# Layer 0's attention on one Trainium2 core, its five instruction queues ordered by a table instead of by a scheduler

## The chip, the cores and the metric

One core of one Trainium2 chip runs the kernel. The core has five engines that work side by side, each through its own queue of instructions and in the order of that queue: TensorE (PE in the profile; its weight loads are PEld), VectorE (DVE), ScalarE (ACT), GpSimd (POOL) and SyncE (SP), which issues the DMA transfers. The metric is the device time of one execution in microseconds (us).

## The reference

Two blocks stand one behind the other, for 1024 tokens of width 1024. The first has two layers (differential attention, then MLA); the second has three mixers and a feed-forward part. The change touches layer 0, which cut to its core is this:

```
h = rmsnorm(x, g) * (1 + scale) + shift          # shift, scale, gate: silu(c) @ ada_w + ada_b
q, k, v, z = split(h @ w_in)                     # w_in 1024 x 4096; 8 heads of 128
q, k = rope(q), rope(k)                          # 2 maps of 64 in each head
sc = einsum('bqhcd,bkhcd->bhcqk', q, k) * scale
p = softmax(sc);  p = p[:, :, 0] - lam * p[:, :, 1]
o = einsum('bhqk,bkhd->bqhd', p, v)
o = rmsnorm(o, subln_g) * (1 - lambda_init) * silu(z)
x = x + gate * (o @ w_out)
```

Layer 1 then starts with its own rmsnorm, shift and scale, and a product with its w_in.

## The kernel before, in words

Products of fp32 numbers are made of three products of a high and a low part each (`mm3`, line 198: hi x hi, hi x lo, lo x hi), so a product of 1024 rows of weights with 512 tokens is 24 matmuls of 512 columns. `wload` (line 185) loads a weight block into a tile wr, casts its high part on ACT (wh, L195) and subtracts the low part on POOL (wl, L181). The activations h are kept as such pairs, in two halves of 512 tokens.

Layer 0's attention goes through 8 heads of 8 tiles (128 queries each), 64 steps (`da_attention`, line 895). A step makes the scores of a tile for both maps (`da_softmax`, line 869: 8 matmuls into two tiles s, a maximum on DVE L760, an exponential on ACT L764, a reciprocal on DVE L879, a scaling on POOL L881, the combination of the two maps on DVE L882). LAG = 2 steps later the tile is transposed on PE (`pt_fill`, L174: 8 transposes, then casts on ACT L783 and subtractions on DVE L181), and after four tiles they are multiplied with v (24 matmuls, `da_stat`), normed (a sum by two matmuls, L410, L411, L920), gated with silu(z) and stored to od by a DMA (L822). Beside that run the products of v and z of the head and of q and k of the next (`qk_rope`, line 637). Its rope is four DVE operations and a POOL addition (L627 to L631); the split pair ab is spread to kk and qq by 32 small DMAs per head (L693). A modulation row of layer 0 and three of layer 1 are summed up in chunks of a loaded weight tile on DVE (L335).

What sets the order: the program hands over its instructions with priorities, and a scheduler puts them on the queues. Only PE's matmuls and transposes are kept in program order there (`self.pin`, `pinned`, line 167); the attention is written ahead by `HP_A` priorities, and generators mix the rest between its steps:

```
fill = alternate(chain(v(h, b2), qk(h + 1, heads[h + 1][0]), z(h, b2)), some(late, 5 if h else 8))
merge(some(att, 8), fill, 0 if h else LEAD0)
```

Behind the last head come the output projection (`out_proj`, line 794; its inputs are the heads loaded back from od by `load_o`, L816 splits them), for half 0 and then half 1, the sum of squares over the result (`stat_sum`, L400), and layer 1's h (`make_h`). There layer 1 starts with two z blocks. PSUM has 8 banks here: two tiles s of two banks, and four tiles m of one bank for all else.

## Time and profile before

| | |
|---|---|
| runs of the kernel before, us | 2951.8 (median of 3; 2949.33 to 2963.5) |
| the profiled execution, us | 2957.26 |
| its span, us (first to last instruction) | 2955.4 |
| mean granted clock of TensorE | 0.949 |
| busy of the span: PE / PEld | 89% / 73% |
| DVE / ACT / POOL | 72% / 48% / 44% |
| mean DMA rate | 115 GB/s |

Times are in us from the start of the span. Layer 0's first scores start at 103, the last head's at 690; its output projection runs from about 776 to 888, layer 1 follows. The granted clock is a share of full speed. A row of a timeline gives start, duration, engine, line, operation, output<-input and count; in brackets stands the idle time of the engine just before, and who ended it.

### The profile page before, as it was taken

How to read it: one execution, taken by the hardware profiler on the slowest of the kernel's cores; microseconds unless marked ns; L12 is line 12 of the kernel's file. 1: busy time of each engine (PE TensorE's matmuls, PEld its weight loads, DVE VectorE, ACT ScalarE, POOL GpSimd, SP SyncE). 2: the span in 40 equal slices, each digit the busy share in tenths (PEclk: the TensorE clock that was granted, in tenths of full speed). 3: DMA queues.
4: the chain of work that ended last, by engine and by line, in shares of the span. 5: the costliest groups of instructions: out<-in, count | busy, mean ns of one | idle time of the engine just before them, and what ended most of it. 6: DMA issues, size and time to landing. Idle time of an engine off the chain costs nothing. (4 is left out here: it accounts for less than half of the span.)

```text
span 2955.4 us, 34418 instructions
## 1 busy us (share of the span) xinstructions
PE 2643.0 (89%) x12023; PEld 2143.1 (73%) x12023; DVE 2117.6 (72%) x2696; ACT 1429.1 (48%) x2609; POOL 1302.3 (44%) x779
## 2 busy tenths in 40 slices
PE   7789999998889989999997798887887999998897
PEld 4667777786768767787775577776775777776775
DVE  7678878776552477676767555568868888889865
ACT  5355545555534544554554344467544444443432
POOL 3333333234244342222233332244537887778761
PEclk8999999999999989999998899999999999998998
DMA  7533433323351264233432336424441222234564
GB/s 269 146 101 83 125 86 85 88 68 111 96 169 58 73 230 137 90 111 94 142 111 69 101 80 91 101 73 117 135 147 50 79 79 75 85 107 154 192 233 145
DMA packets 316849, 338.90 MB, mean 115 GB/s; under 512 B 37684, under 2 KB 240516, under 8 KB 316676
## 3 DMA queue, kind: packets, MB, share of 16 engines
q1 hardware_dynamic: 316676, 336.70, 38.7%
q8 instruction: 96, 1.57, 0.2%
q14 instruction: 77, 0.63, 0.1%
HBM read 231.17 MB, written 60.89 MB: 99 GB/s over the span
## 5 line engine op out<-in xcount | busy, mean ns | idle before, releaser
L171 PE MATMUL m<-h,wh 128*128 128x512 f32 x4744 | 1398.1, 405 | 78.4 <-ACT wh L195 15.8
L171 PEld LDWEIGHTS m<-h,wh 128*128 128x128 f32 x4744 | 915.8, 195 | 288.2 <-ACT wh L195 16.7
L171 PE MATMUL m<-h,wl 128*128 128x512 f32 x1472 | 590.7, 403 | 9.7 <-POOL wl L181 9.7
L181 POOL TENSOR_TENSOR wl<-wr,wh 128x1024 fp32r<-128x1024 f32 (+1 forms) x146 | 328.9, 2259 | 475.6 <-ACT wh L195 144.5
L171 PEld LDWEIGHTS m<-h,wl 128*128 128x128 f32 x1472 | 287.8, 196 | 74.9 <-POOL wl L181 12.1
L783 ACT CAST pt<-m 128x256 fp32r<-128x256 f32 (+1 forms) x632 | 218.6, 373 | 237.9 <-PE m L174 134.7
L764 ACT ACTIVATE e<-s,cf 128x1024 f32<-128x1024 f32 x192 | 215.2, 1122 | 190.8 <-DVE cf L760 87.7
L181 DVE TENSOR_TENSOR pt<-m,pt 128x256 fp32r<-128x256 f32 (+2 forms) x652 | 254.0, 415 | 65.2 <-ACT pt L783 53.5
L760 DVE TENSOR_REDUCE cf<-s 128x1 f32<-128x1024 f32 x192 | 229.6, 1215 | 53.0 <-PE s L171 53.0
L171 PE MATMUL m<-pt,v 128*128 128x512 f32 (+3 forms) x1052 | 240.4, 376 | 15.3 <-ACT pt L1493 9.9
L881 POOL TENSOR_SCALAR e<-e,cf 128x1024 f32<-128x1024 f32 x64 | 84.0, 1313 | 344.9 <-DVE cf L879 291.6
L171 PEld LDWEIGHTS m<-pt,v 128*128 128x128 f32 x1052 | 189.2, 192 | 55.5 <-ACT pt L1493 11.3
L171 PE MATMUL s<-kk,qq 128*128 128x512 f32 (+3 forms) x752 | 191.1, 391 | 41.0 <-DVE e L1417 17.5
L171 PE MATMUL s<-h,wh 128*128 128x512 f32 x720 | 183.7, 401 | 34.3 <-DVE h L181 16.8
L174 PE MATMUL m<-cr,e 128*128 128x128 f32 x1314 | 193.0, 279 | 17.8 <-DVE pt L181 11.6
L1607 DVE SCALAR_TENSOR_TENSOR e<-z,cf,e 128x1023 f32<-128x1023 f32 (+1 forms) x88 | 175.8, 2009 | 24.8 <-ACT e L1605 24.6
L171 PEld LDWEIGHTS s<-kk,qq 128*128 128x128 f32 x752 | 136.8, 198 | 73.5 <-DVE e L1417 20.4
L174 PEld LDWEIGHTS m<-cr,e 128*128 128x128 f32 x1314 | 157.7, 143 | 43.3 <-issue 14.9
L171 PEld LDWEIGHTS s<-h,wh 128*128 128x128 f32 x720 | 137.1, 192 | 70.4 <-DVE h L181 18.5
L171 PE MATMUL s<-h,h 128*128 128x512 f32 x640 | 167.3, 408 | 18.8 <-DVE h L181 11.4
L195 ACT CAST wh<-wr 128x1024 fp32r<-128x1024 f32 (+2 forms) x134 | 122.0, 914 | 112.2 <-PE m L171 48.8
L171 PEld LDWEIGHTS s<-h,h 128*128 128x128 f32 x640 | 121.1, 194 | 49.4 <-DVE h L181 13.3
(343 smaller groups left out, 4087.9 us busy)
## 6 DMA issues: line engine op xcount, KB each, us to landing
wr<-in_w_out_dram SPq DMA_DIRECT2D x48, 512.0 KB
tb<-in_w_ada_dram SPq DMA_DIRECT2D x48, 512.0 KB
wr<-in_w_up_dram SPq DMA_DIRECT2D x47, 512.0 KB
wr<-in_w_in_dram SPq DMA_DIRECT2D x45, 512.0 KB
qq<-ab SPq DMA_DIRECT2D x144, 128.0 KB
wr<-in_ada_w_dram SPq DMA_DIRECT2D x32, 512.0 KB
tf<-act SPq DMA_DIRECT2D x30, 512.0 KB
wr<-in_w_down_dram SPq DMA_DIRECT2D x30, 512.0 KB
```

Of the source, the lines that this page charges most:

```text
L171: return self.pinned(self.nc.tensor.matmul(*args, **kw))
L174: return self.pinned(self.nc.tensor.transpose(*args))
L181: (eng or self.nc.vector).tensor_sub(lo, src, hi.bitcast(F32))
L195: nc.scalar.copy(hi, raw)
L760: nc.vector.reduce_max(nm, ps, axis=AX, negate=True)
L764: nc.scalar.activation(e, ps, AF.Exp, bias=nm, scale=scale, accum_out=sm)
L783: nc.scalar.copy(hi, ps[:, i:i + m])
L881: nc.gpsimd.tensor_scalar(e1, e1, sm[:, 1:2], self.neglam, ALU.mult, ALU.mult)
L1607: nc.vector.scalar_tensor_tensor(t[:, sh:], u[:, 0:S - sh], col(i), t[:, sh:], ALU.mult, ALU.add)
```

## The change

All five engines are wrapped (`Engine`), so that every instruction issued while `self.pin` is set keeps its program order on its queue. `at(g, place, fn)` enters a piece of work in a table under a step g and a place in the step; `run_table` emits the table in the order of steps and places, from step -4 to 82. A product becomes a `unit`: 12 matmuls at place 60, 12 at place 80 of its step, its result read in the next step; the four transposes of each half tile stand at places 50 and 70. v stands in a head's steps 0 and 1, q and k of the next head in steps 2 to 5, z of the next head in steps 6 and 7 (the last head's own v and z in 56 to 59; z of head 0 in steps -2 and -1), and the products with v in step 6 and step 2 of the next head. The output projection takes steps 64 to 79, three z blocks of layer 1 (half 0) steps 80 to 82. Transposes and sums go to two PSUM tiles t, products to two tiles u, in this stretch in place of the four m. wr has 5 buffers where it had 2 (phase 0), wl of phase 1 has 3 where it had 2. The q and k columns of w_in0 are laid out anew by the host, so that one DMA loads q and k of 512 rows in rows of 1 KB, where there were two with 512 bytes, and the cast reads straight. Two small loads of column vectors move to steps 9 and 17. The diff, cut to its core:

```diff
-LEAD0 = 2
...
-    dict(h4=20, kk=5, qq=5, ab=2, pt=12, e=6, v=3, z=3, wr=2, wh=3, wl=3, tb=3, t2=4, tf=3),
-    dict(h4=18, kk=4, qq=6, ab=3, pt=12, e=6, v=3, z=3, wr=4, wh=3, wl=2, tb=3, t2=2, tf=4),
+    dict(h4=20, kk=5, qq=5, ab=2, pt=12, e=6, v=3, z=3, wr=5, wh=3, wl=3, tb=3, t2=4, tf=3),
+    dict(h4=18, kk=4, qq=6, ab=3, pt=12, e=6, v=3, z=3, wr=4, wh=3, wl=3, tb=3, t2=2, tf=4),
...
+    def __getattr__(self, name):
+        f = getattr(self.engine, name)
+
+        def call(*args, **kw):
+            ins = f(*args, **kw)
+            return self.net.tc.keep_in_program_order(ins) if self.net.pin else ins
+
+        return call
...
+    def pt(self, shape=(128, 512)):
+        self.n += 1
+        return self.ps_t.tile(list(shape), F32, tag="t", name=f"t_{self.n}")
+
+    def pu(self, shape=(128, 512)):
+        self.n += 1
+        return self.ps_u.tile(list(shape), F32, tag="u", name=f"u_{self.n}")
...
-            for i, c0 in enumerate((qcol, kcol)):
-                nc.sync.dma_start(
-                    raw[:, :, i], w[g * 512:g * 512 + 512, c0:c0 + 128].rearrange("(k p) m -> p k m", p=128))
-            src = raw.rearrange("p k q (s i f) -> p i (k q s) f", s=2, i=2)
-            h, l = (x.rearrange("p i k (s f) -> p i (k s) f", f=32) for x in (hi, lo))
+            rows = lambda c0, n: w[g * 512:g * 512 + 512, c0:c0 + n].rearrange("(k p) m -> p k m", p=128)
+            if kcol is None:
+                nc.sync.dma_start(raw.rearrange("p k q m -> p k (q m)"), rows(qcol, 256))
+                src = raw.rearrange("p k i m -> p i k m")
+                h, l = hi, lo
+            else:
+                for i, c0 in enumerate((qcol, kcol)):
+                    nc.sync.dma_start(raw[:, :, i], rows(c0, 128))
+                src = raw.rearrange("p k q (s i f) -> p i (k q s) f", s=2, i=2)
+                h, l = (x.rearrange("p i k (s f) -> p i (k s) f", f=32) for x in (hi, lo))
...
+    def at(self, g, place, fn, *args, phase=0):
+        self.table.setdefault(g, []).append((place, len(self.table.get(g, ())), fn, args, phase))
+
+    def run_table(self):
+        self.pin = True
+        for g in range(min(self.table), max(self.table) + 1):
+            for _, _, fn, args, self.phase in sorted(self.table.get(g, ()), key=lambda e: e[:2]):
+                fn(*args)
+        self.pin = False
+        self.phase = 0
...
+    def weight_block(self, g, srcs, chunks, phase=0, late=0):
+
+
+        nc = self.nc
+        ws, box = [], []
+
+        def load():
+            raw = self.load("wr", [128, 1024])
+            for dst, src in srcs(raw):
+                nc.sync.dma_start(dst, src)
+            box.append(raw)
+
+        def first():
+            hi = self.t("wh", [128, 1024], F32R)
+            nc.scalar.copy(hi, box[0])
+            box.append(hi)
+
+        def rest():
+            raw, hi = box
+            lo = self.t("wl", [128, 1024], F32R)
+            self.lo(lo, raw, hi, nc.gpsimd)
+            ws.extend(zip(chunks(hi), chunks(lo)))
+
+        self.at(g - (3 if late < 0 else 2), 11, load, phase=phase)
+        self.at(*((g, 9) if late > 0 else (g - 1 + late, 57)), first, phase=phase)
+        self.at(*((g, 35) if late > 0 else (g - 1 + late, 67)), rest, phase=phase)
+        return ws
...
+    def unit(self, g, ws, rs, read, phase=0, place=10):
+
+        box = []
+
+        def part(i):
+            if i == 0:
+                box.append(self.pu())
+            sl = slice(4 * i, 4 * i + 4)
+            self.mm3(box[0], ws()[sl], rs()[sl], start=i == 0, stop=i == 1)
+
+        self.at(g, 60, part, 0, phase=phase)
+        self.at(g, 80, part, 1, phase=phase)
+        self.at(g + 1, place, lambda: read(box[0]), phase=phase)
...
+            self.unit(g + half, lambda: ws, lambda half=half: hts[half], lambda ps, half=half: read(half, ps))
+            self.at(g + 2, (58, 90)[half], turns, half)
...
+        self.at(g + 2, 90, abs_exp)
+        self.at(g + 3, 58, ln)
+        self.at(g + 3, 91, both)
+        self.at(g + 4, 11, exp)
+        self.at(g + 4, 37, mul)
...
+            for qk in (1, 0):
+                for s in range(2):
+                    for d in range(2):
+                        for i in range(2):
+                            r = slice(64 * d + 32 * i, 64 * d + 32 * i + 32)
+                            x = slice(64 * qk + 32 * s, 64 * qk + 32 * s + 32)
+                            if qk:
+                                self.move(kk[s][r, half * 512:half * 512 + 512], ab[i][x, d])
+                            else:
+                                self.move(q[s][r], ab[i][x])
+
+        for half in range(2):
+            for i in range(2):
+                self.unit(g + 2 * half + i, lambda i=i: [(h[:, i], l[:, i]) for y in ws for h, l in y],
+                          lambda half=half: hts[half], lambda ps, half=half, i=i: read(half, i, ps), place=34)
+            self.at(*((g + 4, 90) if half else (g + 3, 56)), parts, half)
+            self.at(g + 4 + half, 12, moves, half)
...
+        self.at(n, 30, scores)
+        self.at(n, 32, exp, 0)
+        self.at(n, 52, exp, 1)
+        self.at(n, 65, sums)
+        self.at(n + 1, 33, combine)
+        self.at(n + LAG, 50, turns, 0)
+        self.at(n + LAG, 70, turns, 1)
...
+        self.at(g, 55, product)
+        self.at(g + 1, 10, read)
+        if h == 7:
+            self.at(g + 1, 85, sums)
+            self.at(g + 2, 11, ln)
+            self.at(g + 2, 11, exp)
+            self.at(g + 2, 34, scale)
+            self.at(g + 2, 36, gated)
+        else:
+            self.at(g + 2, 45, sums)
+            self.at(g + 2, 51, ln)
+            self.at(g + 2, 59, exp)
+            self.at(g + 2 + 2 * half, 92, scale)
+            self.at(g + 5 - half, 93 + half, gated)
+            self.at(g + 6 - half, 12, put)
...
+        self.at(g, 12, load)
+        self.at(g + 1, 90, keep)
...
+                self.at(g - 1, 96, load, w, grp, k, n)
+                self.at(g, 93, chunk, k, n, name)
+                n += 1
+            self.at(g + 1, 91, end, name, b, grp)
...
+        self.at(g - 2, 12, load)
+        for n in range(8):
+            ws = self.plain_block(g + n, w[:, n * 128:(n + 1) * 128], 0, -1)
+            self.unit(g + n, lambda ws=ws: ws, lambda: ots[half], lambda ps, n=n: read(n, ps))
+            if n % 2:
+                self.at(g + n + 2, 12, store, n)
...
+        self.at(g, 20, parts)
+        self.at(g, 72, sums)
+        for c in range(8):
+            self.at(g + c // per, 90 if per < 8 else 94, chunk, c)
...
+        for h in range(8):
+            g = 8 * h
+            block = lambda i: w[:, i * 1024 + h * 128:i * 1024 + h * 128 + 128]
+            self.da_z(g - 2 if h == 0 else g + 6 if h < 7 else g + 2, block(3), hts, zs[h])
+            self.da_v(g, block(2), hts, vs[h])
+            if h < 7:
+                self.da_qk(g + 2, w, h + 1, hts, kks[h + 1], qts[h + 1])
+            for half in range(2):
+                pts = []
+                for j in range(4):
+                    self.da_tile(g + 4 * half + j, kks[h], lambda h=h, half=half: qts[h][half], pts)
+                self.da_output(h, half, vs[h], pts, zs[h], od, ots)
...
+        steps = [g for g in range(66) if g % 8 in (0, 2, 6, 7)]
+        self.da_mods(steps, cs, [(a["ada_w0"], self.col["ada_b0"], 2, "gate0")] + [
+            (a["ada_w1"], self.col["ada_b1"], i, nme) for i, nme in ((1, "scale1"), (0, "shift1"), (2, "gate1"))])
+        for i, c in enumerate(((0, 1), (2, 3), (4, 5), (6,))):
+            self.da_chunks(56 + i if i < 3 else 62, od, 0, c, ots)
+            self.da_chunks(64 + i, od, 1, c, ots)
...
+        for half, tags in enumerate((("kk", "kk", "ab", "ab"), ("pt",) * 4)):
+            g = 64 + 8 * half
+            self.da_project(g, a["w_out0"], ots, lambda: self.mod["gate0"], xs0, self.xs1, half, tags, acc, xbox[half])
+            self.da_next(g + 8, (3, 8)[half], half, acc, xbox[half], lambda: (cols["a"], self.mod["shift1"]), h1[half])
+        wss, z1 = [], []
+        for i in range(3):
+            g = 80 + i
+            c = 704 + i * 128
+            ws = self.plain_block(g, a["w_in1"][:, c:c + 128], 1, -1)
...
+            self.unit(g, lambda ws=ws: ws, lambda: h1[0], read, 1)
+        self.run_table()
+        return h1, (wss, z1)
...
+    w = given["w_in0"]
+    qk = w[:, :2048].reshape(D, 2, 8, 2, 2, 32).transpose(0, 2, 4, 1, 3, 5).reshape(D, 2048)
+    given["w_in0"] = np.concatenate([qk, w[:, 2048:]], axis=1)
```

Three places, as the queues stand before and now. First PE in step 9 and its like (s scores, cr<-e transposes, h with wh, wl a product). Before:

```order
L171 MATMUL m_1564<-h_84_585,wh_1555 128x512 x2
L171 MATMUL m_1564<-h_84_585,wl_1556 128x512
L171 MATMUL s_1594<-kk_963,qq_1050 128x512 x4
L171 MATMUL s_1602<-kk_964,qq_1059 128x512 x4
L174 MATMUL m_1613<-cr,e_1478 128x128 x4
L174 MATMUL m_1622<-cr,e_1478 128x128 x4
L171 MATMUL m_1631<-h_86_591,wh_1555 128x512 x2
```

With the change:

```order
L111 MATMUL s_1564<-kk_1314,qq_1316 128x512 x4
L111 MATMUL t_1573<-cr,e_1451 128x128 x4
L111 MATMUL u_1586<-h_86_597,wh_1465 128x512 x2
L111 MATMUL u_1586<-h_86_597,wl_1469 128x512
L111 MATMUL u_1586<-h_87_601,wh_1465 128x512 x2
L111 MATMUL u_1586<-h_87_601,wl_1469 128x512
L111 MATMUL u_1586<-h_89_607,wh_1465 128x512 x2
L111 MATMUL u_1586<-h_89_607,wl_1469 128x512
L111 MATMUL u_1586<-h_90_611,wh_1465 128x512 x2
L111 MATMUL u_1586<-h_90_611,wl_1469 128x512
L111 MATMUL t_1603<-cr,e_1451 128x128 x4
L111 MATMUL u_1586<-h_92_617,wh_1465 128x512 x2
```

The two groups of four transposes stood together; now half a product stands between them, and the second half behind them.

Second SP where the second half of the next head's k and q is spread (kk, qq from ab), at the end of a head. Before:

```order
L693 DMA kk_964<-ab_1206 32x512
L693 DMA kk_964<-ab_1207 32x512
L693 DMA qq_1219<-ab_1206 32x1024 x2
L693 DMA qq_1219<-ab_1207 32x1024 x2
L693 DMA qq_1228<-ab_1206 32x1024
L645 DMA wr_1749<-in_w_in_dram 128x4x128 x2
L693 DMA qq_1228<-ab_1206 32x1024
L693 DMA qq_1228<-ab_1207 32x1024
L645 DMA wr_1756<-in_w_in_dram 128x4x128 x2
L693 DMA qq_1228<-ab_1207 32x1024
L325 DMA wr_1788<-in_ada_w_dram 128x1024
L822 DMA od_638<-t_226_1443 128x512
```

With the change (step 7 of head 1):

```order
L111 DMA qq_1978<-ab_1926 32x1024
L111 DMA wr_2102<-in_ada_w_dram 128x1024
L111 DMA od_644<-t_282_1746 128x512
L111 DMA kk_1975<-ab_2093 32x512
L111 DMA kk_1975<-ab_2094 32x512
L111 DMA kk_1975<-ab_2093 32x512
L111 DMA kk_1975<-ab_2094 32x512
L111 DMA kk_1976<-ab_2093 32x512
L111 DMA kk_1976<-ab_2094 32x512
L111 DMA kk_1976<-ab_2093 32x512
L111 DMA kk_1976<-ab_2094 32x512
L111 DMA qq_2113<-ab_2093 32x1024
```

Weight loads stood among the last moves; now a modulation load and the store of a head's output (od) stand ahead of all 16, the 8 of k go first, and nothing stands among them.

Third PE where the sum of squares of layer 0's half 0 is taken (tf,cr), in the output projection. Before:

```order
L171 MATMUL m_6797<-h_1022_6251,wh_6791 128x512 x2
L171 MATMUL m_6797<-h_1022_6251,wl_6792 128x512
L171 MATMUL m_6797<-h_1032_6326,wh_6791 128x512 x2
L171 MATMUL m_6797<-h_1032_6326,wl_6792 128x512
L171 MATMUL m_6797<-h_1055_6431,wh_6791 128x512 x2
L171 MATMUL m_6797<-h_1055_6431,wl_6792 128x512
L171 MATMUL m_6852<-tf_6849,cr 128x512
L171 MATMUL m_6911<-h_1106_6785,wh_6905 128x512 x2
L171 MATMUL m_6911<-h_1106_6785,wl_6906 128x512
L171 MATMUL m_6911<-h_1107_6788,wh_6905 128x512 x2
```

With the change (step 72):

```order
L111 MATMUL u_6867<-h_1084_6571,wl_6806 128x512
L111 MATMUL u_6867<-h_1092_6636,wh_6791 128x512 x2
L111 MATMUL u_6867<-h_1092_6636,wl_6806 128x512
L111 MATMUL u_6867<-h_1093_6639,wh_6791 128x512 x2
L111 MATMUL u_6867<-h_1093_6639,wl_6806 128x512
L111 MATMUL t_6882<-tf_6862,cr 128x512 x2
L111 MATMUL u_6867<-h_1103_6689,wh_6791 128x512 x2
L111 MATMUL u_6867<-h_1103_6689,wl_6806 128x512
L111 MATMUL u_6867<-h_1104_6692,wh_6791 128x512 x2
L111 MATMUL u_6867<-h_1104_6692,wl_6806 128x512
L111 MATMUL u_6867<-h_1111_6737,wh_6791 128x512 x2
L111 MATMUL u_6867<-h_1111_6737,wl_6806 128x512
```

The sum stood ahead of the product of half 1 (its second matmul further down, in that product); both its matmuls now stand in the middle of the product.

## Rows read from the trace of the kernel before

**Rows 1.** Windows: busy (count) of PE, PEld, DVE, ACT, POOL; granted clock; DMA share, GB/s.

```profile
117.00:671.00 554.00, 522.01 (x2476) 429.38 (x2475) 438.50 (x597) 301.21 (x593) 183.58 (x99) 0.98 0.34 92
671.00:776.00 105.00, 88.58 (x400) 71.29 (x399) 74.56 (x103) 64.15 (x125) 35.85 (x20) 0.93 0.35 106
776.00:836.00 60.00, 48.19 (x211) 39.15 (x210) 20.71 (x34) 22.24 (x37) 18.63 (x8) 0.92 0.43 127
836.00:888.00 52.00, 46.74 (x195) 37.52 (x195) 31.86 (x30) 21.97 (x32) 29.50 (x18) 0.96 0.54 162
1060.00:1110.00 50.00, 36.49 (x144) 28.56 (x142) 40.73 (x46) 17.15 (x32) 13.88 (x9) 0.80 0.76 247
```

**Rows 2.** Timeline of PE, 199 to 223 us.

```profile
199.82 1.03 PE L174 MATMUL m<-cr,e 128*128 128x128 f32 x8
200.61 0.72 PE L171 MATMUL m<-h,wh 128*128 128x512 f32 x2
...
208.48 5.61 PE L171 MATMUL m<-pt,v 128*128 128x512 f32 x24
213.93 1.04 PE L174 MATMUL m<-cr,e 128*128 128x128 f32 x8
...
216.60 0.73 PE L171 MATMUL m<-h,wh 128*128 128x512 f32 x2 [0.59 <-DVE v L181]
...
222.18 1.98 PE L171 MATMUL s<-kk,qq 128*128 128x512 f32 x8
```

**Rows 3.** Windows of PE's instructions of line L171 alone (512-column matmuls).

```profile
117.00:671.00 554.00, 477.63 (x1980) 0.98 0.34 92
671.00:776.00 105.00, 79.95 (x310) 0.93 0.35 106
776.00:836.00 60.00, 46.95 (x195) 0.92 0.43 127
```

**Rows 4.** Timeline of PE, 181 to 194 us.

```profile
181.30 3.71 PE L171 MATMUL s<-kk,qq 128*128 128x512 f32 x8
...
190.87 0.99 PE L171 MATMUL m<-h,wh 128*128 128x512 f32 x2 [4.54 <-DVE pt L181]
...
192.09 1.05 PE L171 MATMUL m<-h,wh 128*128 128x512 f32 x2
...
193.37 1.05 PE L171 MATMUL m<-h,wh 128*128 128x512 f32 x2
```

**Rows 5.** Timelines of ACT and of PE at the sum of half 0.

```profile
832.50 1.14 ACT L816 CAST h<-tf 128x512 fp32r<-128x512 f32 x2 [4.82 <-DMA tf<-od]
...
835.58 0.80 PE L171 MATMUL m<-tf,cr 128*128 128x512 f32 x1 [9.42 <-ACT tf L400]
```

**Rows 6.** Timelines of SP (DMA issues), DVE and PE before head 7's first scores.

```profile
677.39 4.99 SPq L693 DMA_DIRECT2D kk<-ab  x8
682.48 4.99 SPq L693 DMA_DIRECT2D qq<-ab  x8
...
684.38 1.28 DVE L882 SCALAR_TENSOR_TENSOR e<-e,cf,e 128x1024 f32<-128x1024 f32 x1
...
690.51 1.98 PE L171 MATMUL s<-kk,qq 128*128 128x512 f32 x8
```

**Rows 7.** Groups by line and shape, 100 to 760 us: busy, mean ns | idle before, releasers.

```profile
L760 DVE TENSOR_REDUCE cf<-s 128x1 f32<-128x1024 f32 x126 | 149.3, 1212 | 14.7 <-PE s L171 14.7
...
L882 DVE SCALAR_TENSOR_TENSOR e<-e,cf,e 128x1024 f32<-128x1024 f32 x62 | 110.0, 1775 | 22.5 <-POOL e L881 22.5
...
L181 DVE TENSOR_TENSOR pt<-m,pt 128x256 fp32r<-128x256 f32 x240 | 93.2, 414 | 24.9 <-ACT pt L783 22.9
...
L881 POOL TENSOR_SCALAR e<-e,cf 128x1024 f32<-128x1024 f32 x62 | 81.6, 1317 | 335.3 <-DVE cf L879 282.0 <-issue 17.6 <-PE s L171 17.5
...
L335 DVE SCALAR_TENSOR_TENSOR t<-wr,cf,t 128x1024 f32<-128x1024 f32 x25 | 34.6, 1385 | 21.1 <-DMA wr<-in_ada_w_dram 21.1
...
L879 DVE RECIPROCAL cf<-cf 128x2 f32<-128x2 f32 x62 | 10.1, 163 | 40.5 <-ACT e L764 40.3
```

More of the change, by code (lines that the diff above doesn't have):

```diff
@@ L108, in __init__ @@
         self.phase = 0
-        self.pin = False
         self.loads = {}
@@ L203, in mm3 @@
             for l, r in ((wh, rh), (wh, rl), (wl, rh)):
-                self.mm(out, l, r, start=start and n == 0, stop=stop and n == last)
+                self.nc.tensor.matmul(out, l, r, start=start and n == 0, stop=stop and n == last)
                 n += 1
@@ L685, in qk_rope, with steps @@
             yield
-        if perm == 1:
-            qf = [lambda hl, j, s=s: qt[s][j // 4][:, hl, (j % 4) * 128:(j % 4) * 128 + 128] for s in range(2)]
-        else:
-            qf = [lambda hl, j, s=s: qt[s][hl][:, j * 128:j * 128 + 128] for s in range(2)]
-        return kk, qf
+        return kk, qt
+    def steps(self, g):
+        while True:
+            try:
+                next(g)
+            except StopIteration as e:
+                return e.value
     def move(self, dst, src):
@@ L713, in v_tiles @@
                 yield
-        late = self.pin and perm == 1
-        if late:
-            for half in range(2):
-                nc.scalar.copy(vt[:, half * 512:half * 512 + 512], self.proj(ws, rs, half))
-                if half == 0:
-                    yield
         for half in range(2):
-            if perm == 1 and not late:
+            if perm == 1:
                 ps = self.proj(ws, rs, half)
@@ new lines, in da_project, with load, read, store @@
+    def da_project(self, g, w, ots, gate, xs_in, xs_out, half, tags, acc, box):
+        nc = self.nc
+        def load():
+            tiles, xt = self.new_xt(tags)
+            box.extend([tiles, xt])
+            self.move_xt(xs_in, half, tiles, False)
+        def read(n, ps):
+            xt = box[1]
+            nc.vector.scalar_tensor_tensor(xt[n], ps, gate()[:, n:n + 1], xt[n], ALU.mult, ALU.add)
+            self.stat_acc(acc()[:, half], xt[n], None, first=n == 0, eng=nc.vector)
+        def store(n):
+            ap = xs_out[(n - 1) * 128:(n + 1) * 128, half * 512:(half + 1) * 512]
+            nc.sync.dma_start(ap.rearrange("(c p) t -> p c t", p=128), box[0][n // 2])
+        self.at(g - 2, 12, load)
[4 more added lines that the diff above has]
+                self.at(g + n + 2, 12, store, n)
@@ L997, in layer0 @@
-        late = chain(
-            self.modulation(cs, a["ada_w0"], self.col["ada_b0"], [(2, "gate0")]),
-            self.modulation(cs, a["ada_w1"], self.col["ada_b1"], [(1, "scale1"), (0, "shift1"), (2, "gate1")]))
-        heads = [(box, [])] + [([], []) for _ in range(7)]
-        ots = [[None] * 8, [None] * 8]
-        att = ahead(self.tc, self.da_attention(heads, od, ots), HP_A)
-        self.pin = True
-        for h in range(7):
-            b2 = heads[h][1]
-            fill = alternate(chain(v(h, b2), qk(h + 1, heads[h + 1][0]), z(h, b2)), some(late, 5 if h else 8))
-            merge(some(att, 8), fill, 0 if h else LEAD0)
@@ L1202, in layer1 @@
         zg = zp()
-        for _ in range(4):
+        for _ in range(3):
             next(zg, None)
```

446 lines of the change are left out of this document (298 added, 148 removed).

## Prediction

> **What bounds the kernel now.** I read the windows of the five engines first, then the matmuls alone in the same windows, then the timeline of TensorE (PE) for what one matmul takes, and last the gaps on PE and who ended them. In the attention of layer 0, 117 to 671 us, PE is busy 522 of 554 us; VectorE (DVE) follows with 438.5, ScalarE (ACT) with 301.2, GpSimd (POOL) with 183.6 [rows 1]. A busy PE is not yet a PE at its best pace, so I count. With its operands there, a product of 24 matmuls of 512 columns runs from 208.48 to 213.93, 0.227 us each, and eight transposes run from 199.82 to 200.61, 0.099 us each [rows 2]. In 117 to 671 stand 1980 of the first kind [rows 3] and 2476 - 1980 = 496 of the second [rows 1], together 1980 x 0.227 + 496 x 0.099 = 498.6 us. So 55.4 us of this stretch are lost: 32 as idle time, and 23.4 as matmuls that ran slowly. The same sum gives 25.7 us lost in the last head (671 to 776: 310 and 90), 14.1 in the first half of the output projection (776 to 836: 195 and 16), 7.7 in the second (836 to 888: 195) [rows 1, 3]. That is 102.9 us, all that this change can win back.
>
> Where it goes is in the gaps. At 190.87 PE had waited 4.54 us for a DVE subtraction, and behind this gap three matmuls take 1.28 us (192.09 to 193.37), 0.427 each: the lower of the two clock levels [rows 4]. At 835.58, where the sum of squares of layer 0's result goes to PE, it had waited 9.42 us; there ACT itself had stood 4.82 us before a copy L816, for a load of the stored heads (tf<-od) [rows 5]. So PE is short of operands, not of time: DVE has 554 - 438.5 = 115 us free, but it meets the work in the wrong order.
>
> **The change part by part.** The matmul count stays. What changes is the order in all five queues, from a table.
>
> *Inside a head.* A tile's step is now scores, four transposes, half a product (12 matmuls), four transposes, the other half, on PE; before, eight transposes stood together and products were whole. A head holds 308 matmuls of 512 columns (64 scores, 48 each for v, z and the products with v, 96 for q and k, 4 sums) and 72 transposes: 308 x 0.227 + 72 x 0.099 = 77.0 us, 0.8 more with the modulation's transposes in half of the heads, so 77.4. Before, head 1's first scores start at 181.30 [rows 4] and head 7's at 690.51 [rows 6]: 84.9 us per head. DVE needs 438.5 / 554 x 84.9 = 67.2 us per head, so it can follow a pitch of 77.4 if its waits stay under 10.2 us. Today it waits for the modulation's weights 21.1 us in all, for the POOL product before the combination 22.5, for the reciprocal's operands 40.5 and before the subtractions of the transposes 24.9 [rows 7], 109 us over 62 tiles, 14 us per head. The first goes: a weight chunk is loaded a step ahead, and wr has five buffers where it had two. The second goes too: the combination stands one step later, behind the next scores. What is left, 65 us or 8.4 per head, is under 10.2, and PE has two steps' worth of banks to bridge it. So I let PE set the pitch inside a head and charge 0.5 us of mixed small waits per head.
>
> *The start of a head is late next.* The second half of the next head's q and k goes through the rope in steps 4 and 5; its split stands at the end of step 6, its 16 moves at the start of step 7, behind a load and the store of a head's output (the order shown above). Eight moves take 4.99 us to issue and what they carry is used at the latest 3.0 us later (687.47 to 690.51) [rows 6]. If the split ends 3 us into step 7 (an estimate: the remainder of DVE's step), the last k arrives at 3 + 0.6 + 5.0 + up to 3.0 = up to 11.6 us, while step 7 gives PE 32 x 0.227 + 8 x 0.099 = 8.1 us. That is up to 3.5 us of waiting at each of seven head starts; since k now goes ahead of q, half of k is there 2.5 us earlier, so below it is 0 to 1. I take 3.0, near the upper end, as DVE's waits push the split later. Kept: 7 x 3.5 = 25; won: 30. Ends: kept 1 per head (48 won) to 7 per head, nearly as before (6 won).
>
> *Moved past SP.* All moves of a half now go without a load between them; before, four loads stood among the last four. The relaid w_in saves SP two issues per head and the casts a strided read: nothing on the path, since ACT has 250 us free in 554 [rows 1]. Of the start (up to the first scores) I expect no change, 4 us either way: DVE gains by having no modulation there, POOL casts z's weights later.
>
> *Head 7.* It has no next head, so z and v fill steps 56 to 59 and then three steps (60, 61 and 63) have only 8 scores and 8 transposes, 2.6 us of PE, against a DVE tile of two maxima, a combination, four subtractions (2 x 1.21 + 1.28 + 4 x 0.41 [rows 6, 7]) plus reads, 5.4 to 6.5 us. PE will idle 3 x 3.4 = 10 us there, and some 5 us more go at the lower clock behind it; projection units that could fill come only at step 64. Kept 15, won 10.7. Ends 0, as now, and 18, with the idle time at DVE's 5.4 us and no cold stretch.
>
> *Projection and seam.* The loads of stored heads now stand at steps 56 to 58, 62 and 64 to 67, ahead of their use by a step, so the 4.82 us before L816 go, and the sum of squares is cut in two: ACT and DVE split it while 12 matmuls (2.7 us) of the next unit run. A split is a cast of 0.57 us on ACT (two in 1.14 [rows 5]) and a subtraction on DVE of the same size, behind an accumulation of two operations; I estimate 3.5 to 4 us with what lies between, so up to 1.5 us is left at each of the two seams. Kept 4 of 14.1 and 2 of 7.7: won 10.1 and 5.7. Ends for both: 7, if only the gap of 9.42 shrinks by the 4.82 of its load and the cold matmuls behind it, and 20.
>
> *Layer 1.* Three z blocks of w_in1 for half 0 stand as cover behind the seam, where two did; the one more is missing as fill later. Before layer 1's first scores PE is busy only 36.5 of 50 us [rows 1]; one half block is 24 x 0.227 = 5.5 us, so this costs 0 to 5.5, and 8 with a cold stretch. I take 2.
>
> **Sum.** 30 + 10.7 + 10.1 + 5.7 - 2 = 54.5 us. The profiled execution took 2957.3 us (span 2955.4), which gives 2902.8; it stood 5.5 us above the median of the runs (2951.8), so **2897 us**. With every end taken together the gain is 1 to 90.
>
> **The rivals.**
> *Smaller gain at the head starts* (0.15). The queue of SP decides: k, q, a store and loads in one file, and a load that waits for its buffer holds the moves behind it. With 7 us kept per head the sum is 6 + 10.7 + 10.1 + 5.7 - 2 = 30.5: 2921 us. For it: 84.9 us per head are largely gaps round the moves. Against: a load has five buffers now.
>
> *The clock* (0.13, with the case that nothing changes). Every step alternates two transposes and two half products between two banks each, so PE may stop shortly several times a step. A fall of the clock cost 1.1 us behind the gap of 4.54 (190.87 to 193.37: 6 matmuls in 2.50 us, 1.36 at full pace [rows 4]); with a stop of as much before it a fall is 2.2 us, and if one comes in every second of 50 steps, 25 x 2.2 = 55 us are paid and the time stays at 2951. Against it: after the gap of 0.59 us at 216.60 a product of 24 goes at full pace, 5.58 us up to 222.18 [rows 2]. The Trainium skill, "TensorE: Matmul & The Clock Gate", section "A second HAM failure mode: psum-queue depth-cycling", describes this very danger, a TensorE that idles briefly between groups while it cycles through PSUM banks and so changes its clock back and forth; the trace of before bears it out for long gaps only. That the table reproduces in effect what the scheduler found (its gaps end on DVE's data, not on its order) ends at the same 2950.
>
> *Slower: DVE becomes the bound* (0.12). The fixed order lets no DVE instruction pass another. A step costs it 8.4 us of work; before, with 1.8 us of waits, that was hidden under 10.6 us. It decides where the waits of one step exceed 2.2 us. With 3.4 us, because each maximum waits for PE and each subtraction for ACT in strict turn, a step is 11.8 and a head 94.4 us: 7 x (94.4 - 84.9) = 66.5 lost, 24.5 won behind the heads: 2957.3 + 42 - 5.5 = 2994 us. For it: the combination takes 1775 ns on average and 1.28 us at best [rows 6, 7], so DVE loses 0.5 us when POOL works beside it, and POOL's place is now fixed as well. Against: the waits for weights and for POOL's product are gone. If each combination waited out a whole POOL multiplication (1317 ns [rows 7]) instead of those 0.5 us, a head would cost DVE 67.2 + 8 x 0.8 = 73.6 us and with 8.4 us of waits 82.0, against the forecast's 77.4 + 3.5 = 80.9: 2897 + 7 x 1.1 = 2905, still faster. The Trainium skill, "SBUF — State Buffer", section "Who interferes with whom", says more: a VectorE operation with two SBUF inputs and a GpSimd operation that reads SBUF lock each other out for the whole instruction, whoever issues first. The stretched combination agrees with it, and the sum by this rule is that 2905.
>
> *Larger gain* (0.05): 1 us per head start and a filled head 7: 2870 us.
>
> **How the numbers follow.** The forecast case, 2880 to 2925, has 0.55. A measurement of this kernel tells changes above 0.5%, 14.8 us: faster means below 2937, slower above 2966.6. Faster is 0.55 + 0.15 + 0.05 and a part of the others, 0.76; within, 0.12; slower, 0.12. The range takes in the smaller and the larger gain and most of the case of no change, and leaves out the slower rival: 2865 to 2950. Its likeliest part is 2880 to 2925.
>
> **What would show it.** Right: in the changed profile a pitch of 80 to 82 us from head to head, full pace between head starts, one gap of 2 to 4 us on PE at each head's first scores that ends on a DMA kk<-ab, idle time in steps 60, 61 and 63, no gap over 3 us where layer 0's sums go to PE, no wait of DVE for wr. Wrong: PE gaps in every step that end on DVE's maxima or subtractions and DVE busy over 85% (the slower rival); a granted clock under 0.95 in the heads without long gaps (the clock); head starts of 7 us (SP); or more idle time before layer 1's first scores than 20 us in place of the 13.5 of now.

## The result, and the profile after

| | before | after |
|---|---|---|
| runs, us | 2956.6 (median of 4; 2949.3 to 2963.5) | 2916.5 (median of 4; 2909.0 to 2923.6) |
| ratio after to before | | 0.9864, 95% interval 0.9821 to 0.9908 |
| the profiled execution / its span, us | 2957.3 / 2955.4 | 2909.9 / 2907.9 |

The kernel is faster by 1.4%, 40 us, inside the range (2865 to 2950); the two profiled executions differ by 47.3 us, where 54.5 were forecast. Single executions of one kernel spread by up to 21 us here, so causes below are read from stretches of the traces.

The first stretches after, as windows (stretch, length, busy us and count of PE, PEld, DVE, ACT and POOL, granted clock, DMA); they run from the first scores of head 0, 1, 7, the last scores, the first sum of layer 0, to the second. They are the counterpart of [rows 1].

```profile
104.09:168.01 63.92, 59.60 (x289) 48.96 (x287) 50.74 (x69) 35.41 (x69) 21.64 (x12) 1.00 0.27 71
168.01:659.66 491.65, 483.04 (x2306) 393.83 (x2307) 384.34 (x548) 274.20 (x552) 165.61 (x91) 0.99 0.35 97
659.66:723.89 64.23, 56.82 (x269) 45.46 (x268) 50.98 (x69) 43.99 (x87) 17.94 (x11) 0.97 0.49 151
723.89:794.86 70.97, 62.70 (x275) 50.33 (x273) 50.79 (x63) 32.41 (x59) 27.09 (x12) 0.93 0.54 162
794.86:846.07 51.21, 47.06 (x194) 37.24 (x194) 26.77 (x28) 22.30 (x32) 27.08 (x19) 0.97 0.56 158
```

The same windows of the kernel before, between the same points of its work:

```profile
103.12:181.30 78.18, 67.40 (x294) 53.62 (x295) 57.35 (x73) 35.85 (x67) 20.38 (x13) 0.89 0.44 117
181.30:690.51 509.21, 484.30 (x2307) 399.18 (x2306) 402.01 (x549) 279.85 (x557) 179.09 (x93) 0.98 0.35 94
690.51:761.05 70.54, 58.71 (x268) 47.48 (x266) 48.14 (x66) 43.41 (x82) 17.71 (x11) 0.93 0.27 84
761.05:835.58 74.53, 59.08 (x255) 47.21 (x253) 33.45 (x51) 31.92 (x58) 23.28 (x11) 0.91 0.44 135
835.58:887.63 52.05, 46.78 (x195) 37.57 (x195) 31.96 (x30) 22.39 (x32) 29.50 (x18) 0.96 0.54 161
```

Taking from each length its matmuls (0.227 us for a matmul, 0.099 for a transpose, counted in the traces) leaves what PE lost there. A matmul of fewer than 512 columns is counted like one of 512; these stand in the first and the last row alone, which therefore show too small a loss, before as after. "Won" is the loss before less the loss after.

| stretch | lost before, us | after | won | forecast |
|---|---|---|---|---|
| up to the first scores | 43.7 | 45.2 | -1.5 | 0 |
| head 0 | 19.1 | 5.7 | 13.4 | |
| heads 1 to 6 | 44.5 | 26.8 | 17.7 | 30 with head 0 |
| head 7 to its last scores | 18.4 | 11.6 | 6.8 | |
| from there to the first sum | 20.4 | 13.3 | 7.1 | 20.8 with head 7 |
| to the second sum | 8.0 | 7.2 | 0.8 | 5.7 |
| on to the end of MLA's attention | 63.3 | 72.4 | -9.1 | -2 |
| layer 1's output projection | 26.0 | 17.9 | 8.1 | 0 |
| mixers | 82.6 | 78.1 | 4.5 | 0 |

So heads 0 to 6 gave what was forecast, and the last head with the seam (from there to the second sum) about half of it. PE's longest waits in heads 1 to 6 before (waiting engine, tile and line, releaser: us in total, times, longest):

```profile
PE m L174 <- DVE pt L181: 8.0, 4, 3.0
PE m L171 <- DVE v L181: 7.6, 4, 3.2
PE m L171 <- DVE pt L181: 6.1, 3, 4.5
```

All three end on DVE's subtractions behind groups of transposes, and none of PE's waits in this stretch ended on a move of k or q. These 21.7 us are gone. What is still lost stands at another place than forecast. PE's waits after, up to head 7's first scores:

```profile
PE t L111 <- ACT t L111: 7.4, 7, 2.1
PE s L111 <- ACT e L111: 4.2, 1, 4.2
PE u L111 <- POOL wl L111: 0.7, 1, 0.7
PE s L111 <- DMA kk<-ab: 0.4, 1, 0.4
```

No start of the heads 1 to 6 waits more than 0.4 us for k; head 7's waits 1.1 us (at 662.24, behind this stretch). The 4.2 us end at head 1's first scores, so they are part of head 0's 5.7: step 7 of head 0 is the one step of the heads 0 to 6 without a product, since z of a head stands in its own steps 6 and 7 (not the next head's, as the section on the change has it) and only head 0's stands ahead of the loop. The gaps of 2.1 us come 8 us behind the first scores of heads 1, 3 and 5. Timelines of SP, POOL, DVE, ACT and PE around head 3's start:

```profile
326.90 4.95 SPq L111 DMA_DIRECT2D kk<-ab  x8
...
333.10 2.39 POOL L111 TENSOR_TENSOR wl<-wr,wh 128x1024 fp32r<-128x1024 f32 x1
...
333.76 2.81 DVE L111 SCALAR_TENSOR_TENSOR t<-wr,cf,t 128x1024 f32<-128x1024 f32 x1
336.49 2.34 DVE L111 TENSOR_REDUCE cf<-s 128x1 f32<-128x1024 f32 x2
...
337.80 1.12 ACT L111 ACTIVATE e<-s,cf 128x1024 f32<-128x1024 f32 x1 [4.25 <-DVE cf L111]
...
339.42 0.71 ACT L111 ACTIVATE t<-t,cf 128x512 f32<-128x512 f32 x1
...
332.21 1.99 PE L111 MATMUL s<-kk,qq 128*128 128x512 f32 x8
...
340.19 0.66 PE L111 MATMUL t<-cr,e 128*128 128x128 f32 x4 [2.08 <-ACT t L111]
```

A modulation chunk on DVE meets POOL's low part of v's weights and takes 2.81 us (1.29 us when it is alone, below); the maxima come late, with them the exponential and, behind it on ACT, the read of the sums (339.42), and PE waits for the PSUM tile that these hold. The chunk is as slow (2.80 to 2.81 us) at the start of every head from 1 to 6, but only heads 1, 3 and 5 pay for it; what spares the even heads was not followed.

### The profile page after: what moved, and what is told of

It reads as the page before. It is cut to its first block, busy times and chain, and to the rows that moved or that the text cites. A ratio compares the mean times of both kernels' runs of the same rounds, so it can differ in the third digit from the quotient of the medians.

```text
span 2907.9 us, 34523 instructions
## 1 busy us (share of the span) xinstructions
PE 2629.5 (90%) x12023; PEld 2128.7 (73%) x12023; DVE 2099.3 (72%) x2696; ACT 1421.6 (49%) x2609; POOL 1292.2 (44%) x779
## 5 line engine op out<-in xcount | busy, mean ns | idle before, releaser
L111 PE MATMUL m<-h,wh 128*128 128x512 f32 x3480 | 985.0, 402 | 48.1 <-DVE h L111 14.4
L111 PEld LDWEIGHTS m<-h,wh 128*128 128x128 f32 x3480 | 669.4, 194 | 204.2 <-DVE h L111 18.2
L111 PE MATMUL u<-h,wh 128*128 128x512 f32 x1264 | 408.3, 404 | 1.4 <-ACT h L111 0.8
L111 PE MATMUL m<-h,wl 128*128 128x512 f32 x840 | 336.8, 402 | 7.8 <-POOL wl L111 7.8
L111 ACT CAST wh<-wr 128x1024 fp32r<-128x1024 f32 (+3 forms) x252 | 202.6, 810 | 170.1 <-PE m L111 67.7
L111 PEld LDWEIGHTS u<-h,wh 128*128 128x128 f32 x1264 | 233.1, 191 | 47.5 <-ACT h L111 1.2
L111 PE MATMUL u<-h,wl 128*128 128x512 f32 x632 | 252.5, 400 | 12.7 <-POOL wl L111 12.7
L111 ACT CAST pt<-m 128x256 fp32r<-128x256 f32 (+2 forms) x396 | 140.1, 376 | 155.1 <-PE m L111 88.4
L111 PEld LDWEIGHTS m<-h,wl 128*128 128x128 f32 x840 | 164.1, 195 | 44.5 <-POOL wl L111 9.0
L111 PE MATMUL s<-h,h 128*128 128x512 f32 x640 | 171.5, 414 | 20.8 <-DVE h L111 14.3
L111 DVE TENSOR_TENSOR pt<-m,pt 128x256 fp32r<-128x256 f32 (+2 forms) x396 | 155.0, 416 | 41.6 <-ACT pt L111 34.6
L111 PEld LDWEIGHTS s<-kk,qq 128*128 128x128 f32 x752 | 135.9, 196 | 65.8 <-DVE e L111 20.4
```

What stands on the lines that cost most here:

```text
L111: ins = f(*args, **kw)
```

## The experiments

"Six heads" is the time from head 1's to head 7's first scores (509.2 before, 491.7 after), read from the one profiled execution of each run. e4, e8 and e11 leave the order in these heads as it is and took 491.8 to 493.3, so differences under 2 us say nothing. The medians come from four to ten executions; each run's ratio is to executions of the kernel before that were timed beside it (medians 2957 to 2961). Each expectation names a theory and a rival to it.

| run | us, median | ratio to before, interval | six heads, us |
|---|---|---|---|
| the changed kernel | 2916.5 | 0.9864, 0.9821 to 0.9908 | 491.7 |
| e1, only PE held | 2903.0 | 0.9816, 0.9790 to 0.9842 | 487.4 |
| e2, wr 2 | 2923.8 | 0.9880, 0.9856 to 0.9904 | 498.4 |
| e3, chunk in step 4 | 2897.8 | 0.9800, 0.9771 to 0.9830 | 482.2 |
| e4, last z later | 2917.7 | 0.9861, 0.9842 to 0.9879 | 492.1 |
| e5, e1 with eight transposes together | 2943.5 | 0.9945, 0.9926 to 0.9963 | 517.3 |
| e6, shared PSUM tiles | 2899.0 | 0.9793, 0.9757 to 0.9829 | 481.6 |
| e7, e3 with a free tail | 2895.2 | 0.9775, 0.9741 to 0.9809 | 481.7 |
| e8, two z blocks | 2909.7 | 0.9825, 0.9784 to 0.9866 | 491.8 |
| e9, e3 + e6 + e7 + e8 | 2899.4 | 0.9795, 0.9773 to 0.9817 | 480.7 |
| e10, eight transposes, all held | 2976.6 | 1.0054, 1.0036 to 1.0072 | 543.9 |
| e11, wl 2 | 2897.9 | 0.9788, 0.9765 to 0.9811 | 493.3 |
| e12, q ahead of k | 2947.5 | 0.9974, 0.9956 to 0.9993 | 523.2 |

**e1.** Which queues' order matters?

```diff
-            return self.net.tc.keep_in_program_order(ins) if self.net.pin else ins
+            return self.net.tc.keep_in_program_order(ins) if self.net.pin and self.pinned else ins
...
-        self.tensor, self.vector, self.scalar = Engine(net, nc.tensor), Engine(net, nc.vector), Engine(net, nc.scalar)
+        self.tensor, self.vector, self.scalar = Engine(net, nc.tensor, True), Engine(net, nc.vector), Engine(net, nc.scalar)
...
-    dict(h4=20, kk=5, qq=5, ab=2, pt=12, e=6, v=3, z=3, wr=5, wh=3, wl=3, tb=3, t2=4, tf=3),
+    dict(h4=20, kk=5, qq=5, ab=2, pt=12, e=6, v=3, z=3, wr=3, wh=3, wl=3, tb=3, t2=4, tf=3),
```

> The table stays as the order in which the program writes its work, but only TensorE is held to it; the four other queues are left to the scheduler (wr has 3 buffers instead of 5, since the scheduler's order keeps more tiles alive). Theory (the order on the feeding queues is what helps): PE waits in the heads again; head 1's to head 7's first scores take 505 to 520 us instead of 491.7, and the run takes 2935 to 2965 us. Rival (PE's own order, half products between the transposes, is what helps): 488 to 496 us for these six heads and 2905 to 2925 us.

The rival came true. With four queues free the kernel is no slower: 2903.0 us, six heads 487.4. Head 0 is longer (76.5 us for 63.9), the start shorter (98.6 for 104.1), head 7 takes 68.2 us for 64.2, and from the last scores to the first sum it takes 61.8 us where the changed kernel takes 71.0. Holding DVE, ACT, POOL and SP is not where the gain of heads 1 to 6 comes from; head 0's gain does hang on it (12.6 us; against that the start is 5.5 us shorter with free queues).

**e5 and e10.** What in PE's order, then? Both move the second four transposes of a tile (and their casts) up to the first four, ahead of a whole product; e5 on top of e1, e10 on top of the changed kernel.

```diff
-        self.at(n + LAG, 70, turns, 1)
+        self.at(n + LAG, 50, turns, 1)
```

> As e1 (only TensorE held to the table, wr 3), but a tile's eight transposes stand together again, ahead of a whole product of 24, as before the change. Theory (the half product between the two groups of transposes gives ACT and DVE time to empty a bank, so that the other queues need no fixed order): the six heads go from 487.4 us in e1 back to 496 to 509 and the run to 2912 to 2928. Rival (where the products stand in the steps is what helps, not their halves): 482 to 491 us and 2897 to 2910.

> The changed kernel, all five queues held, with only the second four transposes moved back to the first four, ahead of the whole product. Theory (the half product between them is the part that helps, as e5 against e1 showed with free queues): six heads take 505 to 525 us instead of 491.7 and the run 2930 to 2955. Rival (held queues make up for it): 490 to 500 us, 2915 to 2925.

The theory came true both times, and past the expected size: six heads take 30 us more than in e1 with free queues, and 52 more than in the changed kernel with held ones, which is then slower than before. PE's waits in e10's heads:

```profile
PE u L111 <- DVE pt L111: 23.9, 11, 3.6
PE u L111 <- DVE tf L111: 9.2, 3, 3.2
PE t L111 <- ACT e L111: 5.9, 7, 1.4
```

PE stands at the start of products, for DVE's subtractions of the transposes; their own operands (h and wh) do not come from these. One such wait, rows of DVE and of PE:

```profile
312.08 1.41 DVE L111 TENSOR_TENSOR pt<-t,pt 128x256 fp32r<-128x256 f32 x4
...
312.97 1.03 PE L111 MATMUL u<-h,wh 128*128 128x512 f32 x2 [3.61 <-DVE pt L111]
```

It ends behind the second of the four subtractions, when the first group of four is read out. I read it as a wait for the PSUM tile that this group still holds. But products have two tiles u of their own, and that it is the tile was not tried by itself, so this cause stays open.

e5 loses at another place, with 21.1 of its 30 us:

```profile
PE t L111 <- DVE cf L111: 21.1, 5, 8.0
```

Three of these waits (8.0, 5.9 and 5.9 us, at 284.35, 456.62 and 626.47) stand in heads 2, 4 and 6, behind the eight transposes that end a modulation row: these fill both tiles t, and the attention's next transposes wait until DVE, in the scheduler's order, has summed them up (cf<-t). With the split, in e1, this wait does not come.

So the one line that splits a product round two groups of transposes is worth more, in this kernel, than the six heads' whole gain, by two different waits. Before the change eight transposes stood together too, but on the four shared tiles m, and the heads took 509.2 us, less than in e5 (517.3). What eight would cost on shared tiles (e6's edit with e5's or e10's) was not run, so the price of 30 or 52 us holds for two tiles t.

**e12.** The order of the moves on SP, of which the forecast made its main term.

```diff
-            for qk in (1, 0):
+            for qk in (0, 1):
```

> Among the 16 moves of a half, the 8 of q go ahead of the 8 of k. Theory (the prediction's sum at the head start: 5.0 us for 8 moves, up to 3.0 us to land): the last k lands 5 us later, PE waits 3 to 6 us on kk<-ab at each of the heads 1 to 7, six heads take 510 to 530 us instead of 491.7, 2935 to 2960 us. Rival (the moves have room, as the missing gaps of the changed kernel suggest): under 1 us per head, 2912 to 2922.

The theory came true: 31.5 us more in six heads, 2947.5 us. PE's waits from head 1 on:

```profile
PE s L111 <- DMA kk<-ab: 30.7, 14, 3.9
PE s L111 <- ACT e L111: 4.2, 1, 4.2
```

The mechanism is there and has just enough room in the changed kernel. At head 3 the moves start at 326.90, as forecast 2.9 us into step 7 (its scores start at 323.98), and k's issue ends at 331.85; the scores of the second map, which need the last of it, start at about 333.1 and wait for nothing. e12 shows how long it takes, at head 3 again, in rows of SP and PE:

```profile
343.70 5.02 SPq L111 DMA_DIRECT2D kk<-ab  x8
...
350.26 1.19 PE L111 MATMUL s<-kk,qq 128*128 128x512 f32 x2 [1.42 <-DMA kk<-ab]
```

What k carries is in use 1.5 us after its issue ends (348.72 to 350.26), not up to 3.0.

**e2.** The five buffers of wr.

```diff
-    dict(h4=20, kk=5, qq=5, ab=2, pt=12, e=6, v=3, z=3, wr=5, wh=3, wl=3, tb=3, t2=4, tf=3),
+    dict(h4=20, kk=5, qq=5, ab=2, pt=12, e=6, v=3, z=3, wr=2, wh=3, wl=3, tb=3, t2=4, tf=3),
```

> wr back from 5 to 2 buffers, all else as changed. Theory (buffers matter since SP is held to its order): a load that waits for its buffer holds the moves of k and q behind it on SP; PE waits at head starts on kk<-ab or on wh, six heads take 505 to 540 us instead of 491.7, 2930 to 2970 us. Rival (the loads are early enough with two): within 5 us of the changed kernel, no new gap over 1 us on PE.

The result lies between the two: 6.8 us more in the six heads, 2.8 in the last. The theory's wait is there, at a small size: PE waits ten times for k, 10.4 us in all and at most 2.0, where the changed kernel waited 0.4, while its wait for the sums' tile falls from 7.4 us to 1.7.

**e3 and e6.** The gaps of heads 1, 3 and 5, from their two sides: DVE's lateness, and the PSUM tile.

```diff
-        steps = [g for g in range(66) if g % 8 in (0, 2, 6, 7)]
+        steps = [g for g in range(66) if g % 8 in (0, 2, 4, 6)]
```

> The modulation chunk of a head's last step moves to step 4 of the head. Theory (at the head's start this chunk meets POOL's low part of v's weights, takes 2.8 us in place of 1.3 and so makes the maxima, the exponentials and ACT's read of the sums late): the gaps of 2.1 us at the second transposes of heads 1, 3 and 5 and the slow matmuls behind them go, these heads take 79.5 to 81 us instead of 83.2 to 83.9, in all 9 to 12 us less. Rival (those transposes wait for the bank of the sums, whose read stands behind an exponential on ACT, whatever DVE does): the gaps stay at 1.5 to 2 us and the time within 3 us.

```diff
-        return self.ps_t.tile(list(shape), F32, tag="t", name=f"t_{self.n}")
+        return self.ps_m.tile(list(shape), F32, tag="m", name=f"m_{self.n}")
...
-        return self.ps_u.tile(list(shape), F32, tag="u", name=f"u_{self.n}")
+        return self.ps_m.tile(list(shape), F32, tag="m", name=f"m_{self.n}")
```

> All queues held to the table as changed, but transposes, sums and products draw on the four shared PSUM tiles m, in place of two t and two u. Theory (order, not banks): six heads within 4 us of 491.7 and 2910 to 2922 us. Rival (own banks keep a product from waiting for a reader of transposes): 496 to 515 us, gaps on PE in most steps, 2922 to 2945.

Either cure alone takes the gaps away: e3 9.5 us, e6 10.1 us less in the six heads, 2897.8 and 2899.0 us. e6 fits neither expectation: tiles of their own for transposes and for products are not neutral, they cost. In e3 POOL's operation stands in the same place at head 3's start, and DVE goes on to its maxima without a chunk; a chunk one step later, alone, takes 1.29 us (timelines of POOL, DVE and PE):

```profile
332.22 2.41 POOL L111 TENSOR_TENSOR wl<-wr,wh 128x1024 fp32r<-128x1024 f32 x1
...
332.88 2.35 DVE L111 TENSOR_REDUCE cf<-s 128x1 f32<-128x1024 f32 x2
...
341.12 1.29 DVE L111 SCALAR_TENSOR_TENSOR t<-wr,cf,t 128x1024 f32<-128x1024 f32 x1 [1.10 <-DMA wr<-in_ada_w_dram]
...
337.29 0.60 PE L111 MATMUL t<-cr,e 128*128 128x128 f32 x4
```

**e4.** The last head's steps without a product.

```diff
-            self.da_z(g - 2 if h == 0 else g + 6 if h < 7 else g + 2, block(3), hts, zs[h])
+            self.da_z(g - 2 if h == 0 else g + 6 if h < 7 else g + 3, block(3), hts, zs[h])
```

> The last head's two z units stand in steps 59 and 60 instead of 58 and 59. Theory (in steps 60, 61 and 63 PE has nothing but scores and transposes and waits for DVE): one of the three holes is filled, head 7 up to its eighth scores takes 60 to 62 us instead of 64.2, 2 to 5 us less in all. Rival (DVE sets the pace in all of head 7): within 1 us.

Inconclusive: head 7 takes 62.8 us (64.2), the stretch behind it 72.9 (71.0); what the filled step wins is lost again behind it, and both differences are small.

**e7.** e3, and the feeding queues free from step 56.

```diff
+            self.loose = g >= 56
...
-            return self.net.tc.keep_in_program_order(ins) if self.net.pin else ins
+            return self.net.tc.keep_in_program_order(ins) if self.net.pin and (self.pinned or not self.net.loose) else ins
```

> e3 (chunk in step 4), and from step 56, the last head, only TensorE is held to the table. Theory (the fixed order of the feeding queues helps at the first head and costs in the last head and at the seam, where e1 lost less): heads 1 to 6 as in e3 (482 us), from head 7's eighth scores to layer 0's first sum 60 to 64 us instead of 71, 2883 to 2892 us in all. Rival (the scheduler's better tail comes from its earlier start, not from its order there): 69 to 72 us and 2895 to 2901.

For the stretch the theory came true: 60.8 us from the last scores to the first sum, where PE lost 13.3 us and now loses 3.2. In the changed kernel the second matmul of the sum for the last head's first half (its low part, step 63) waits 4.22 us, behind a modulation chunk that takes 3.36 us against POOL's wl, and behind a gate, all in fixed order; the next transposes wait another 2.66 us behind the same chain. PE's and DVE's rows there, changed kernel:

```profile
727.15 3.36 DVE L111 SCALAR_TENSOR_TENSOR t<-wr,cf,t 128x1024 f32<-128x1024 f32 x1
730.43 0.68 DVE L111 TENSOR_TENSOR t<-t,z 128x512 f32<-128x512 f32 x1
...
731.77 0.80 PE L111 MATMUL t<-tf,cr 128*128 128x512 f32 x1 [4.22 <-DVE tf L111]
```

and the same sum in e7:

```profile
718.02 0.47 PE L111 MATMUL t<-tf,cr 128*128 128x512 f32 x1 [0.27 <-ACT pt L111]
719.65 0.51 PE L111 MATMUL t<-tf,cr 128*128 128x512 f32 x1 [1.17 <-DVE tf L111]
```

The median, 2895.2, is 3 us under e3's and above the range given: the 10 us of the stretch do not show in the whole time. It is the lowest median of the study, but not told apart from e3, e6, e9 and e11.

**e8 and e11.** What layer 1 lost: the third z block, or its wl buffers?

```diff
-        for i in range(3):
+        for i in range(2):
...
-            for hs in ((0, 1, 2), (3,), (4,), (5,), (6,), (7,)):
+            for hs in ((0, 1), (2,), (3,), (4,), (5,), (6,), (7,)):
...
-        for _ in range(3):
+        for _ in range(2):
```

> Two z blocks of layer 1 as cover at the seam, as before, the third goes back to layer 1's fill. Theory (the third block is missing as fill in MLA's attention, which lost 64.9 us instead of 53): layer 1's attention gets back 8 to 12 us of loss, the seam loses 0 to 4, 2905 to 2912 us. Rival (the longer attention is chance of that one execution, as e2's 462 us with the same fill says): no gain, 2914 to 2922.

```diff
-    dict(h4=18, kk=4, qq=6, ab=3, pt=12, e=6, v=3, z=3, wr=4, wh=3, wl=3, tb=3, t2=2, tf=4),
+    dict(h4=18, kk=4, qq=6, ab=3, pt=12, e=6, v=3, z=3, wr=4, wh=3, wl=2, tb=3, t2=2, tf=4),
```

> Layer 1's wl back from 3 to 2 buffers, all else as changed. Theory (the 8 us won in layer 1's output projection come from this buffer: before, PE waited twice 7.5 to 8.3 us there for a cast of weights): that stretch takes 68 to 71 us again instead of 62.4, 2920 to 2928 us. Rival (they come from another order of the scheduler behind the moved z block): 61 to 64 us, 2912 to 2920.

e8 is inconclusive: from the second sum to the end of MLA's attention PE loses 68.7 us (72.4 after, 63.3 before). One trace each does not settle a difference of that size: e2 and e4 ran MLA's attention with the same order on PE, DVE, ACT and POOL, and took 462.2 and 468.9 us. e11 is a miss for its theory and a find: layer 1's output projection keeps its gain (61.2 us), so that does not come from wl; but the attention takes 454.3 us instead of 472.2, with the same 2146 matmuls, and all four executions (2893 to 2901) lie under the fastest of the changed kernel. MLA's attention, changed kernel and then e11:

```profile
1028.79:1500.95 472.16, 437.74 (x2146) 358.63 (x2146) 333.64 (x626) 230.46 (x514) 122.45 (x98) 0.96 0.39 122
```

```profile
1031.70:1486.00 454.30, 431.17 (x2146) 355.43 (x2146) 320.38 (x623) 229.60 (x512) 116.58 (x95) 0.97 0.40 122
```

The twelve traces with three wl buffers took 462 to 472 us there, and the changed kernel's is the longest of them; the kernel before, with two, took 460.3. So a third wl buffer lets the scheduler order layer 1 otherwise, and worse, by 8 to 18 us; a closer figure the traces do not give. Which instruction it moves was not followed; nor were the projection's 8 us and the mixers' 4.5, which only traces of other orders of the scheduler show.

**e9.** Four of these edits together.

> Four edits together: chunk in step 4 (e3), shared PSUM tiles (e6), the feeding queues free from step 56 (e7), two z blocks as cover (e8). Theory (they act at different places, but e3 and e6 cure the same gap): heads 1 to 6 in 478 to 483 us, layer 0's end as e7, 2878 to 2892 us. Rival (with shared banks and free queues the tail loses again what e7 won): 63-rd scores to the first sum 68 to 73 us, 2893 to 2902.

The time is the rival's, 2899.4, but not for its reason. The heads take 480.7 us and the stretch to the first sum 60.8, as in e7, but the last head 69.8 instead of e7's 64.5; e3 and e6 cure the same gap, so nothing is added there. e11's edit with e7's was not tried.

## Why the prediction was right, and where not

*The bound and the size.* PE's loss by counting, 102.9 us in 117 to 888, was the right quantity: the granted clock in heads 1 to 6 rose only from 0.98 to 0.99, PE's busy time hardly changed (484.3 and 483.0 us), and the six heads are 17.6 us shorter nearly all by idle time. Heads 0 to 6 won 31.1 us, where 30 were forecast, but that is in part luck. The forecast's stretch, 117 to 671 us, had lost 55.4 us, the two rows here, 103 to 690, had lost 63.6; what they still lose is 32.5 us, where the forecast kept 25. And head 0 gave 13.4 of the 31.1; heads 1 to 6, which still lose 4.5 us each instead of 3.5, gave only 17.7. The pitch was 80.3 to 80.7 us in the even heads, inside the 80 to 82 of the forecast, and 83.2 to 83.9 in the odd ones.

*The reason given for it failed.* "DVE meets the work in the wrong order", cured by holding the queues: e1 has the gain of heads 1 to 6 without holding them. What this gain needs is a sentence that the text passed over without a price, "half a product (12 matmuls), four transposes, the other half": undone, with the casts and subtractions that move along, it costs 30 us (e5) or 52 (e10). Holding the queues makes this split needed more, not less. The waits that the change removed, 21.7 us behind DVE's subtractions, fit that. Not tried by itself were eight transposes on shared tiles and the relaid w_in, so the split is shown as needed, not as the only cause.

*The start of a head* was charged 3.0 us, from a landing of up to 3.0 us. PE waited 0.4 us for k in heads 1 to 6 and 1.1 us at head 7; the landing took 1.5 us (e12). Nor did it hold that "84.9 us per head are largely gaps round the moves": no wait of PE in heads 1 to 6 of the kernel before ended on them. The price of the other order was right: e12's 31.5 us are 5.3 per head. The forecast came out near because a wait that it did not have, for the tile of the sums, took the place (e3 and e6 both remove it): heads 1, 3 and 5 still lose 6.2 to 6.7 us, the even ones 2.4 to 2.8.

*The rivals.* The clock did not cycle with the two tiles each: it was granted at 1.00 and 0.99 in the heads. So the danger that the Trainium skill, "TensorE: Matmul & The Clock Gate", section "A second HAM failure mode: psum-queue depth-cycling", describes is not seen in this trace. DVE did not become the bound (384 of 492 us), and its waits for the modulation's weights and for POOL's product are gone, as forecast. The combination and the chunk in 103 to 720 us:

```profile
L111 DVE SCALAR_TENSOR_TENSOR e<-e,cf,e 128x1024 f32<-128x1024 f32 x61 | 93.7, 1536 | 0.0
...
L111 DVE SCALAR_TENSOR_TENSOR t<-wr,cf,t 128x1024 f32<-128x1024 f32 x26 | 44.8, 1722 | 0.0
```

The combination's mean fell from 1775 ns to 1536, the chunk's rose from 1385 to 1722. Both take 1.28 us alone. From the first scores to 745 us eighteen of them, nine of each kind, ran beside an operation of POOL and took 2.1 to 3.5 us; every one ended 1.07 to 1.09 us behind POOL's. At the starts of heads 1, 3 and 5 and in step 63 it was a chunk, and PE paid for it (2.80 to 2.81 and 3.36 us). This agrees with the Trainium skill, "SBUF — State Buffer", section "Who interferes with whom", by which a VectorE operation with two SBUF inputs contends for one port with a GpSimd operation that reads SBUF. The 2905 us for that rule let the combination wait for its own multiplication on POOL; what was met instead was the low part of weights and the product of z.

*Head 7 and the seam* were oversized: 26.5 us forecast, 14.7 won. "ACT and DVE split it while 12 matmuls run" held for layer 0's sums (waits of 0.2 to 0.3 us). The step that failed is that nothing else was charged there: the last head's own sum, of its first half, stood behind a chunk, with 4.22 and 2.66 us of waits, and that is about what head 7 and the first half of the projection won less (13.9 for 20.8). The second half gave 0.8 for 5.7; POOL's wl comes late there (1.37 and 1.93 us), the rest was not followed.

*Layer 1* was charged for the z block, 2 us; its attention lost 9.1 in the traces. A buffer count that the sum left out cost 8 to 18 us there (e11); whether the z block cost anything e8 does not tell.

## What to carry to other kernels

When an engine works through groups that others must empty, look first at what stands between two groups on its own queue: splitting a product round them was worth more here than fixing the order of four other queues. A fixed order must then keep apart what slows each other down, here DVE operations on two SBUF tiles and POOL's. And price every number that a diff changes, buffer counts of another stage too, since a scheduler answers to them far from the edit.

## What was not expected of the hardware

A DVE operation of 1.28 us took 2.81 and 3.36 us beside one of POOL of 2.39 and 2.78, and ended 1.08 us behind it each time. Eight small moves were issued in 5.02 us and their last data was in use 1.5 us later.
